# Where ScalarE's and VectorE's share of an activation pair's sums stands in the queue of a fused decoder layer

## The chip, the cores and the metric

The kernel runs on one core of one Trainium2 chip. The metric is the device time of one execution in microseconds (us). A core has five engines with queues of their own, each of which takes its instructions strictly in the order in which the program lists them: TensorE (PE, matrix products), VectorE (DVE), ScalarE (ACT), GpSimd (POOL) and SyncE (SP, which here only issues loads). They wait for each other through semaphores. Transfers between HBM and the on-chip memory run on DMA engines beside them, whoever issues them.

## The reference, cut to what matters

One decoder layer over 272 tokens (16 meta tokens and 256 of the input), model width 2048. The first part projects the input, computes a sparse attention for half of the width and a causal pooling for the other half, mixes both with `w_o` and normalises. The change lies in what follows, a gated feed-forward block (FFN) of width 5632 and a last layer norm:

```python
def conv_gated_ffn(h, w_up, conv_w, conv_b, w_down):
    T = h.shape[1]
    z = h @ w_up
    zp = jnp.pad(z, ((0, 0), (CONV_WIDTH - 1, 0), (0, 0)))
    z = sum(zp[:, j:j + T] * conv_w[j] for j in range(CONV_WIDTH)) + conv_b
    a, g = jnp.split(z, 2, axis=-1)
    return (jax.nn.gelu(a) * g) @ w_down
...
        f = conv_gated_ffn(h, w_up[l], conv_w[l], conv_b[l], w_down[l])
        h = layer_norm(ALPHA * h + f, ln2_g[l], ln2_b[l])
```

Everything is float32.

## The kernel before, in words

**Weights come as blocks.** All weights stream through the kernel as 128 x 2048 blocks of 1 MB, in the order of the list `stream`. `weights()` hands out the block with the index `state["use"]` and first calls `emit` for the blocks up to two ahead of it. `emit` takes a raw buffer (three of them, tag `wraw`) and a split buffer (three, tag `whl`) and calls `fetch` (line 109): SyncE issues the load (L110), and then the block is split into a high and a low half in a shorter float format, in two pieces of 1024 columns. For each piece ACT copies the high half (L123) and DVE subtracts it from the raw block for the low half (L124). A product is then three matmuls for each 128 rows: high x high, high x low and low x high (L187, L188, L189). The load of the block three further on waits until DVE has read the last of the raw buffer; the split of the block three further on waits until PE has done with the split buffer.

**The FFN goes by tiles f = 0 to 43**, each with two halves: half 0 is the value column block `a`, half 1 the gate column block `g`, one weight block each. For f = 0 to 3 (`FOLDED`) the layer norm before the FFN is not yet applied to the activations; it is folded into the product and undone behind it by `unfold` (a DVE copy L707, a DVE product L709, an ACT multiply L711 and a POOL add L712). Then `conv` does the convolution (ACT L699, DVE L700 and L701) and `gate` the activation and the product (ACT L716, DVE L717). From f = 4 on the normalised activations are used.

**The down product** is done with fewer multiplications for parts 0 to 3 and half of part 4: activations and weights are taken in 2 x 2 blocks and seven products of sums replace eight (`seven`). The sums of the weights are made by DVE in `fetch` (L115, L118 to L120). The sums of the activations are made by `forms(r, j, whole)` (from line 729), once for a pair of tiles f: four POOL additions and subtractions into the buffer `forms` (L736 to L739), and then high and low halves of the results by `two_parts`, ACT L722 and DVE L723, four times. A finished pair goes into the list `todo`. At the start of a later tile half, when the block of that half has been handed out, `forms` is called for the first pair in `todo`, if `f > FOLDED - 1 + half_`. So the pairs (0, 1) and (2, 3) are taken at f = 4 half 0 and f = 5 half 0, and each later pair right after its second tile.

**Other work around it.** Behind f = 4 and f = 5, eight DVE transposes each (L861) turn the residual; from f = 6 on, `residual` issues 32 small DMAs from ACT's queue (L693), each of which needs all 16 transposes.

**The end.** The last part (four tiles f) is multiplied plainly, and the row mean of the layer norm comes out of the product itself: each of the last four blocks gets an extra column with the sum of its rows. `row_sums` (line 173) makes it: ACT sums the raw block in place (L176), ACT writes the high half of the sum (L178), DVE the low half (L179). The call for the very last block stands earlier, in the `down` branch. The other three calls stand behind the loop that hands out the last blocks, followed by two ACT sums over `y2`, the running output (L886), one for each half i of the tokens. Then PE makes five pieces for i = 0 and five for i = 1 (L928 to L930); DVE adds each to `y2` (L932); the piece `MEAN` carries the row sums, and L935 makes the negative mean from it. ACT squares follow (L896), DVE subtracts the mean (L902), scales (L917), and the result goes out. The scale and offset rows come as eight loads that POOL issues (L876), each behind a tiny POOL copy (L875) that waits for the last block's load.

**What sets the order.** The program is written in one order, but the framework's scheduler lists the instructions of each engine by priority and readiness as it models them. An instruction that the scheduler thinks ready may therefore be listed ahead of one that the text has before it. Semaphores are added afterwards.

Of the kernel before, what the change touches and what calls it, by code (L numbers as in the profile page):

```python
# [2 lines left out]

# [1 line left out]

# [6 lines left out]
F32 = mybir.dt.float32  # L12
F32R = mybir.dt.float32r
AF = mybir.ActivationFunctionType
ALU = mybir.AluOpType
# [20 lines left out]
FAST = 4  # L36
FOLDED = 4
# [30 lines left out]
def tile_layer(ctx, tc, xt, w_first, w_proj, w_uk, w_uv, w_pool, w_o, w_up, w_down, cols, rows, rel_bias, onehot, out):  # L68
    nc = tc.nc
# [21 lines left out]
    stream = [w_proj[j] for j in range(8)] + [w_uk, w_uv] + [w_proj[j] for j in range(8, 24)]  # L91
    stream += [w_o[j] for j in range(KT)]
    plan = ffn_plan()
    kinds = {}
# [8 lines left out]
            stream.append(w_down[sum(PARTS[:item[1]]) + item[2] * (PARTS[item[1]] // 2) + item[3]])  # L103
    stream += [w_down[d] for d in range(FT - PARTS[-1], FT)]
    spare, last = len(stream) - PARTS[-1], len(stream) - 1
    ready, raws = {}, {}
    state = {"next": 0, "use": 0}

    def fetch(raw, hl, src, kind=None):
        nc.sync.dma_start(raw, src)  # L110
        b11, b12, b21, b22 = (raw[:, c:c + 512] for c in range(0, 2048, 512))
        cuts = (0, 1024, 2048)
        if kind == "A":

            nc.vector.tensor_tensor(b12, b12, b11, op=ALU.subtract)  # L115
        if kind == "B":

            nc.vector.tensor_tensor(b12, b22, b12, op=ALU.subtract)  # L118
            nc.vector.tensor_tensor(b11, b12, b11, op=ALU.add)  # L119
            nc.vector.tensor_tensor(b21, b21, b11, op=ALU.subtract)  # L120
            cuts = (0, 1024, 1536)
        for c in (slice(a, b) for a, b in zip(cuts, cuts[1:])):
            nc.scalar.activation(hl[:, 0, c], raw[:, c], AF.Copy)  # L123
            nc.vector.tensor_tensor(hl[:, 1, c], raw[:, c], hl[:, 0, c].bitcast(F32), op=ALU.subtract)  # L124

    def weight_tiles():
        raw = wp.tile([P, 2048], F32, tag="wraw", name="wraw")
# [2 lines left out]
    def emit(i):  # L130
        if i in ready:
            return
        if i == last:

            raw = wp.tile([P, 2048], F32, tag="wraw", name="wraw")
            nc.sync.dma_start(raw, stream[i])
            raws[i] = raw
            ready[i] = []
            for c in range(0, 2048, 256):
                hl = ring.tile([P, 2, 258], F32R, tag="act", name="whl_r", padded_shape=[P, 2, T])  # L140
                nc.scalar.activation(hl[:, 0, :256], raw[:, c:c + 256], AF.Copy)
                nc.vector.tensor_tensor(hl[:, 1, :256], raw[:, c:c + 256], hl[:, 0, :256].bitcast(F32), op=ALU.subtract)
                ready[i].append(hl)
            return
        if i == spare:
            raw = wp.tile([P, 2048], F32, tag="wraw", name="wraw")
            hl = sb.tile([P, 2, 2048 + 2], F32R, tag="y", name="whl_y")
        else:
            raw, hl = weight_tiles()
        fetch(raw, hl, stream[i], kinds.get(i))  # L150
        ready[i] = hl
        if i >= spare:
            raws[i] = raw
# [6 lines left out]
    def weights(ahead=2):  # L160
        i = state["use"]
        state["use"] += 1
        prefetch(i + 1 + ahead)
        return ready.pop(i)

    def pieces(hl, a, b):

# [5 lines left out]
    def row_sums(i, hl):  # L173

        total = sb.tile([P, 1], F32, name=f"total{i}")
        nc.scalar.activation(raws[i], raws[i], AF.Copy, accum_out=total)  # L176
        hi, lo = (hl[-1][:, p, 256:] if isinstance(hl, list) else hl[:, p, 2048:] for p in range(2))
        nc.scalar.activation(hi, total.to_broadcast([P, 2]), AF.Copy)  # L178
        nc.vector.tensor_tensor(lo, total.to_broadcast([P, 2]), hi.bitcast(F32), op=ALU.subtract)  # L179
# [552 lines left out]
    def forms(r, j, whole):  # L732

        a11, a21, a12, a22 = r[:, 0, :P], r[:, 0, P:], r[:, 1, :P], r[:, 1, P:]
        s = fp.tile([P, 4 * P], F32, name="forms", tag="acc", bufs=1).rearrange("p (a b) -> p a b", b=P)
        nc.gpsimd.tensor_tensor(s[:, 0], a21, a22, op=ALU.add)  # L736
        nc.gpsimd.tensor_tensor(s[:, 2], s[:, 0], a11, op=ALU.subtract)
        nc.gpsimd.tensor_tensor(s[:, 1], a12, s[:, 2], op=ALU.subtract)
        nc.gpsimd.tensor_tensor(s[:, 3], a11, a21, op=ALU.subtract)  # L739
        left = two_parts(slot(), r[:, :, :P])  # L740
        mid = two_parts(slot(), s[:, :2])
        right = ring.tile([P, 2, T], F32R, tag="act", name="right")
        right = two_parts(right[:, :, :2 * P].rearrange("p a (b c) -> p a b c", c=P), s[:, 2:])
        if j % 2 == 0:
            held["lone"], held["other"] = slot(), slot() if whole else None
        two_parts(held["lone"][:, :, j % 2], a22)
        if whole:
            two_parts(held["other"][:, :, j % 2], a21)
        return {"P1": (left, 0), "P2": (left, 1), "P5": (mid, 0), "P3": (mid, 1), "P6": (right, 0),
                "P7": (right, 1), "P4": (held["lone"], j % 2),  # L750
                "a11": (left, 0), "a12": (left, 1), "a21": (held["other"], j % 2), "a22": (held["lone"], j % 2)}
# [44 lines left out]
    for item in plan:  # L796
        if item[0] in "AB":
            seven(*item)
            continue
        if item[0] == "down":  # L800
            _, part, c, g = item
            hl = weights()
            if c == 1:
                emit((last, spare)[g])
                if g == 0:
                    row_sums(last, ready[last])
            if g == 0:
                downs = [big(), big()]
            n = PARTS[part]
            for k in range(4 * g, 4 * g + 4):  # L810
                w = slice(512 * (k - 4 * g), 512 * (k - 4 * g) + 512)
                for i in range(2):
                    a, r = pairs[part][k // 2][f"a{i + 1}{k % 2 + 1}"]
                    nc.tensor.matmul(downs[i], a[:, 0, r], hl[:, 0, w], start=k == 0, stop=False)
                    nc.tensor.matmul(downs[i], a[:, 0, r], hl[:, 1, w], start=False, stop=False)
                    nc.tensor.matmul(downs[i], a[:, 1, r], hl[:, 0, w], start=False, stop=k == n - 1)
            if g == n // 4 - 1:
                for i in range(2):
                    yc = y2[:, i, 512 * c:512 * c + 512]
                    nc.vector.tensor_tensor(yc, yc, downs[i], op=ALU.add)  # L820
            continue
        _, f, half_ = item
        part = next(p for p in range(len(PARTS)) if f < sum(PARTS[:p + 1]))
        if half_ == 0:
            if f % 2 == 0:
                pair = fp.tile([P, 2, S], F32, name="za", tag="z0", bufs=3)
            both = []
        hl = weights()
        ps = big()
        if todo and f > FOLDED - 1 + half_:  # L830
            p, r = todo.pop(0)
            pairs[p].append(forms(r, len(pairs[p]), p == FAST))
        if f < FOLDED:
            k = 0
            if f + half_ == 0:
                product(ps[:, :NE], hl, P, folded, 0, NE, k1=7)
                deviation()
                product(ps[:, :NE], hl, P, folded, 0, NE, k0=7, k1=14)
                deviation_rows()
                k = 14  # L840
            product(ps[:, :NE], hl, P, folded, 0, NE, k0=k)
            while len(h_parts) < min(KT, 3 * (2 * f + half_ + 1)):
                normalise(len(h_parts))
            both.append(ps)
            if half_ == 0:
                continue
            both = [conv(i * FT + f, i, unfold(both[i]), pair[:, f % 2]) for i in range(2)]
        else:
            product(ps[:, :NQ], hl, P, h_parts, 0, NQ)
            both.append(conv(half_ * FT + f, half_, ps, pair[:, f % 2]))  # L850
            if half_ == 0:
                continue
        gate(*both)
        if part > FAST:
            a = fp.tile([P, 2, NE], F32R, name="gp", tag="gp", bufs=16)
            gated.append(two_parts(a[:, :, :S], both[0]))
        elif f % 2:
            todo.append((part, pair))
        if f in (FOLDED, FOLDED + 1):
            for m in range(8 * (f - FOLDED), 8 * (f - FOLDED) + 8):  # L860
                nc.vector.transpose(y[:, m, NM:], y[:, m, NM:])  # L861
        if FOLDED + 2 <= f < FOLDED + 8:
            for _ in range((6, 5, 5)[f % 3]):
                residual(*moves.pop(0))
# [11 lines left out]
            nc.gpsimd.dma_start(t, rows[r:r + 1, 512 * c:512 * c + 512].to_broadcast([P, 512]))  # L876
            gb.append(t)
    order = [0, n - 1] + list(range(1, n - 1))
    for k in range(n - 1):
        row_sums(spare + k, hls[k])  # L880
    MEAN = (1792, 2048 + 2)
    cuts = [[(0, 512), (512, 1024), (1024, 1536), MEAN, (1536, 1792)], [MEAN, (0, 512), (512, 1024), (1024, 1536), (1536, 1792)]]
    mvs = [fp.tile([P, 12], F32, name="mv", tag=f"mv{i}", bufs=1) for i in range(2)]
# [133 lines left out]
```

## Time and profile before

| | us |
|---|---|
| median of 3 runs | 1053.46 |
| lowest and highest run | 1052.87, 1053.99 |
| the profiled execution's own time | 1052.47 |
| its span, first to last instruction | 1050.7 |
| PE busy in the span | 1036.6 (99%) |
| DVE busy | 889.6 (85%) |
| ACT busy | 621.0 (59%) |
| POOL busy | 214.8 (20%) |
| mean granted TensorE clock | 0.997 of full speed |

How to read the rows that follow: a row of the timeline gives the start and the duration in us, the engine, the line of the kernel, the operation, the tile that it writes and those that it reads, shapes where they matter, and in brackets the idle time ahead of it with what ended it. `ACTq` and `SPq` are the queues' own instructions, such as the issue of a DMA. Matmuls overlap, since they are pipelined, so the distance from one start to the next tells more than the duration. A row of the waits gives who waited for whom, the total in us, how often, and the longest.

### The profile page before, as it was taken

Reading aid. Unit: us, or ns where it says so; the run is one execution under the profiler, and the core shown is the slowest. Engines: PE = TensorE matmul, PEld = TensorE weight load, DVE = VectorE, ACT = ScalarE, POOL = GpSimd, SP = SyncE. Lnnn points to the kernel's source line nnn. Section 1 sums busy time; section 2 is a strip of 40 time slices with the busy share of each in tenths; the row PEclk is TensorE's granted clock in tenths of the full one; section 3 lists DMA queues with packets and bytes.
Section 4 is the critical chain, followed back from the end, with each engine's and each line's share of the span. In section 5 each row is a group of like instructions: output and inputs, shape, how many; then the busy total and the mean of one; then the engine's idle time right before and its main releaser. Section 6 shows DMA issues by size and latency. Waiting matters only on the chain. (4 is left out here: it accounts for less than half of the span.)

```text
span 1050.7 us, 19241 instructions
## 1 busy us (share of the span) xinstructions
PE 1036.6 (99%) x7671; PEld 986.5 (94%) x7671; DVE 889.6 (85%) x1381; ACT 621.0 (59%) x998; POOL 214.8 (20%) x264
## 2 busy tenths in 40 slices
PE   9999999999999999999999999999999999999996
PEld 8998999999999999999999999999999999999985
DVE  6879468858779987898989989899898998989876
ACT  7566346745447765565555655556555665556673
POOL 1100014125436231201112011120111221220040
PEclk9999999999999999999999999999999999999998
DMA  8756542454552577998788787887878778787763
GB/s 324 256 170 241 189 152 93 149 188 166 191 199 83 201 221 207 284 311 271 269 288 273 282 276 268 283 278 278 276 268 289 272 279 275 274 284 264 285 218 133
DMA packets 59322, 249.75 MB, mean 238 GB/s; under 512 B 21686, under 2 KB 22112, under 8 KB 32224
## 3 DMA queue, kind: packets, MB, share of 16 engines
q1 hardware_dynamic: 34160, 229.76, 60.3%
q0 software_dynamic: 7600, 15.62, 7.9%
q10 hardware_dynamic: 17472, 3.15, 1.6%
q8 instruction: 60, 0.98, 0.4%
q14 instruction: 30, 0.25, 0.1%
HBM read 232.50 MB, written 2.11 MB: 223 GB/s over the span
## 5 line engine op out<-in xcount | busy, mean ns | idle before, releaser
L124 DVE TENSOR_TENSOR whl<-wraw,whl 128x1024 fp32r<-128x1024 f32 (+1 forms) x416 | 489.6, 1212 | 45.1 <-ACT whl L123 44.5
L123 ACT ACTIVATE whl<-wraw 128x1024 fp32r<-128x1024 f32 (+1 forms) x416 | 402.3, 1015 | 103.5 <-DVE wraw L119 22.5
L188 PE MATMUL mm<-hp,whl 128*128 128x258 f32 x1280 | 362.4, 283 | 0.0
L187 PE MATMUL mm<-hp,whl 128*128 128x258 f32 x1280 | 362.0, 283 | 0.3 <-ACT whl L123 0.3
L189 PE MATMUL mm<-hp,whl 128*128 128x258 f32 x1280 | 361.1, 282 | 0.8 <-DVE whl L124 0.8
L187 PEld LDWEIGHTS mm<-hp,whl 128*128 128x128 f32 x1280 | 242.4, 189 | 3.7 <-ACT whl L123 0.5
L188 PEld LDWEIGHTS mm<-hp,whl 128*128 128x128 f32 x1280 | 242.5, 189 | 3.1
L189 PEld LDWEIGHTS mm<-hp,whl 128*128 128x128 f32 x1280 | 242.9, 190 | 1.0 <-DVE whl L124 1.0
L187 PE MATMUL mm<-xp,whl 128*128 128x256 f32 (+5 forms) x384 | 111.8, 291 | 0.0
L188 PE MATMUL mm<-xp,whl 128*128 128x256 f32 (+5 forms) x384 | 108.9, 284 | 0.0
L189 PE MATMUL mm<-xp,whl 128*128 128x256 f32 (+5 forms) x384 | 108.7, 283 | 0.0
L699 ACT ACTIVATE z<-mm,cv 128x256 f32<-128x256 f32 x40 | 22.6, 565 | 97.3 <-PE mm L189 96.4
L188 PEld LDWEIGHTS mm<-xp,whl 128*128 128x128 f32 x384 | 72.3, 188 | 0.8 <-issue 0.5
L187 PEld LDWEIGHTS mm<-xp,whl 128*128 128x128 f32 x384 | 72.4, 189 | 0.6
L189 PEld LDWEIGHTS mm<-xp,whl 128*128 128x128 f32 x384 | 72.4, 189 | 0.3 <-DVE whl L124 0.2
L739 POOL TENSOR_TENSOR forms<-za 128x128 f32<-128x128 f32 x20 | 26.4, 1321 | 219.4 <-DVE za L717 211.9
L765 PE MATMUL at<-whl,gp 128*128 128x512 f32 x180 | 71.2, 395 | 0.0
L766 PE MATMUL at<-whl,gp 128*128 128x512 f32 x180 | 71.1, 395 | 0.0
L764 PE MATMUL at<-whl,gp 128*128 128x512 f32 x180 | 71.1, 395 | 0.0
L699 ACT ACTIVATE za<-mm,cv 128x256 f32<-128x256 f32 x40 | 22.5, 564 | 67.4 <-PE mm L189 67.4
L736 POOL TENSOR_TENSOR forms<-za 128x128 f32<-128x128 f32 x20 | 21.8, 1088 | 106.4 <-DVE za L717 106.3
L766 PEld LDWEIGHTS at<-whl,gp 128*128 128x128 f32 x180 | 33.8, 188 | 8.0
(327 smaller groups left out, 1942.2 us busy)
## 6 DMA issues: line engine op xcount, KB each, us to landing
wraw<-in_w_up SPq DMA_DIRECT2D x88, 1024.0 KB, 5.1
wraw<-in_w_down SPq DMA_DIRECT2D x80, 1024.0 KB, 6.3
wraw<-in_w_proj SPq DMA_DIRECT2D x24, 1024.0 KB, 5.0
wraw<-in_w_o SPq DMA_DIRECT2D x16, 1024.0 KB, 4.9
y<-v POOLq DMA_DIRECT2D x27, 256.0 KB, 8.3
y<-u POOLq DMA_DIRECT2D x18, 256.0 KB, 4.7
wraw<-in_w_first SPq DMA_DIRECT2D x8, 304.0 KB, 5.5
x<-in_xt SPq DMA_DIRECT2D x1, 2176.0 KB, 8.6
```

What stands on the lines that cost most here:

```text
L123: nc.scalar.activation(hl[:, 0, c], raw[:, c], AF.Copy)
L124: nc.vector.tensor_tensor(hl[:, 1, c], raw[:, c], hl[:, 0, c].bitcast(F32), op=ALU.subtract)
L187: nc.tensor.matmul(ps, wh, ah, start=n == 0, stop=False)
L188: nc.tensor.matmul(ps, wh, al, start=False, stop=False)
L189: nc.tensor.matmul(ps, wl, ah, start=False, stop=n == KT - 1)
L699: nc.scalar.activation(z, src[:, 2:NQ], AF.Identity, bias=col(C_B, j), scale=col(C_W, 3 * j + 2))
L736: nc.gpsimd.tensor_tensor(s[:, 0], a21, a22, op=ALU.add)
L739: nc.gpsimd.tensor_tensor(s[:, 3], a11, a21, op=ALU.subtract)
L764: nc.tensor.matmul(ps, a[:, 0, i], hl[:, 0, w], start=j == 0, stop=False)
L765: nc.tensor.matmul(ps, a[:, 0, i], hl[:, 1, w], start=False, stop=False)
L766: nc.tensor.matmul(ps, a[:, 1, i], hl[:, 0, w], start=False, stop=j == n - 1)
```

## The change

`fetch` returns the last ACT and the last DVE instruction of a split, and `emit` keeps them for each block in `split`. A new context `behind(i)` makes every ACT instruction traced in it be listed after that ACT instruction of block i, and every DVE instruction after that DVE instruction; this is an order in the queues alone and adds no semaphore. `forms` is called within `behind(state["use"])`, so behind the split of the block that the next tile half will use, and the condition for it becomes `f > FOLDED + half_`. The three calls of `row_sums` at the end stand within `behind(spare + n - 2)`, the last block that is split in whole pieces.

```diff
             nc.vector.tensor_tensor(b21, b21, b11, op=ALU.subtract)
             cuts = (0, 1024, 1536)
         for c in (slice(a, b) for a, b in zip(cuts, cuts[1:])):
-            nc.scalar.activation(hl[:, 0, c], raw[:, c], AF.Copy)
-            nc.vector.tensor_tensor(hl[:, 1, c], raw[:, c], hl[:, 0, c].bitcast(F32), op=ALU.subtract)
+            upper = nc.scalar.activation(hl[:, 0, c], raw[:, c], AF.Copy)
+            lower = nc.vector.tensor_tensor(hl[:, 1, c], raw[:, c], hl[:, 0, c].bitcast(F32), op=ALU.subtract)
+        return upper, lower
...
-        fetch(raw, hl, stream[i], kinds.get(i))
+        split[i] = fetch(raw, hl, stream[i], kinds.get(i))
...
+    @contextmanager
+    def behind(i):
+
+        upper, lower = (getattr(ins, "ins", ins) for ins in split[i])
+        with tc.issue_after(upper), tc.issue_after(lower):
+            yield
...
-        if todo and f > FOLDED - 1 + half_:
+        if todo and f > FOLDED + half_:
             p, r = todo.pop(0)
-            pairs[p].append(forms(r, len(pairs[p]), p == FAST))
+            with behind(state["use"]):
+                pairs[p].append(forms(r, len(pairs[p]), p == FAST))
...
-    for k in range(n - 1):
-        row_sums(spare + k, hls[k])
+    with behind(spare + n - 2):
+        for k in range(n - 1):
+            row_sums(spare + k, hls[k])
```

The lists of PE and of SyncE stay as they are, instruction for instruction. ACT's and DVE's lists hold the same work in another order, in these places:

- Pair (0, 1): its four ACT and four DVE instructions stood around the split of the block for f = 5 half 0; they now stand behind the split of the block for f = 5 half 1. Pair (2, 3): it stood on both sides of the split for f = 5 half 1; it now stands behind the split for f = 6 half 1.
- The last DVE transpose (L861) moves ahead, to the place that the first low half (L723) had ahead of the split for f = 5 half 0. The first two residual DMAs (L693) move ahead of the ACT split for f = 5 half 1, and the last of the 32 moves ahead by one tile half.
- In POOL's list two additions of pair (2, 3) change places, and one output accumulation (L789) of part 0 moves behind three POOL additions. On DVE, in part 0, L786 (which frees a PSUM bank of `seven`) moves behind a split and an L772, and three splits change places with a neighbour.
- Two 128 x 128 high and low halves of part 4's pairs move behind the next split.
- At the end ACT's list was: split of block 1 of the last four, L176 of it, split of block 2, L178, split of block 3, L176, L886, L178, L176, L886, L178. It becomes: split 1, split 2, split 3, then L176, L176, L178, L176, L178, L886, L178, L886. On DVE the low halves of the sums (L179) change places with the first additions L932 accordingly.

More of the change, by code (lines that the diff above doesn't have):

```diff
@@ L1 @@
 import math
[L2 removed]
+from contextlib import ExitStack, contextmanager
 import numpy as np
```

3 lines of the change are left out of this document (1 added, 2 removed).

## The prediction

> **What bounds the kernel now.** I read the page first, then the windows, PE's waits, and the timeline around each wait.
>
> ```profile
> span 1050.7 us, 19241 instructions
> ```
> ```profile
> 500.00:600.00 100.00, 100.00 (x719) 94.55 (x718) 92.52 (x129) 58.69 (x83) 16.17 (x19) 1.00 0.81 278
> ```
> ```profile
> PE mm L189 <- DVE whl L124: 1.2, 2, 0.8
> ```
>
> PE bounds everything up to the last 30 us, in this stretch without a gap and at full granted clock (1.00). PE's list doesn't change, so a change of ACT's and DVE's order is worth only what PE waits for, or what it makes PE wait for. PE's waits on low halves come to 1.2 us in this view, which is short, because a pipelined matmul counts as busy until its modelled end. The distance between starts shows the loss. Only two places hold such a loss near the instructions that move: the block for f = 5 half 1, and the last four blocks.
>
> ```profile
> 374.06 0.29 PE L188 MATMUL mm<-hp,whl 128*128 128x258 f32 x1
> 374.19 0.28 PE L189 MATMUL mm<-hp,whl 128*128 128x258 f32 x1
> 374.74 0.39 PE L187 MATMUL mm<-hp,whl 128*128 128x258 f32 x1 [0.27 <-ACT whl L123]
> 374.97 0.28 PE L188 MATMUL mm<-hp,whl 128*128 128x258 f32 x1
> 376.06 0.39 PE L189 MATMUL mm<-hp,whl 128*128 128x258 f32 x1 [0.82 <-DVE whl L124]
> 376.29 0.28 PE L187 MATMUL mm<-hp,whl 128*128 128x258 f32 x1
> ```
>
> Undisturbed starts are 0.12 us apart. From 374.19 to 376.29 four steps took 2.10 us instead of 0.48: 1.62 us are lost. First the high half is late, then the low half.
>
> **Part 1: the pairs (0, 1) and (2, 3).** Why was that split late? Here are ACT's, DVE's and POOL's timelines.
>
> ```profile
> 367.93 0.60 ACT L699 ACTIVATE z<-u,cv 128x256 f32<-128x256 f32 x1 [0.78 <-POOL u L712]
> 370.88 0.42 ACT L722 ACTIVATE gp<-forms 128x256 fp32r<-128x256 f32 x1 [2.35 <-POOL forms L738]
> ...
> 372.86 0.42 ACT L722 ACTIVATE gp<-za 128x256 fp32r<-128x256 f32 x1 [1.05 <-DVE za L717]
> 373.19 0.55 ACT L699 ACTIVATE za<-mm,cv 128x256 f32<-128x256 f32 x1
> 373.64 2.00 ACT L123 ACTIVATE whl<-wraw 128x1024 fp32r<-128x1024 f32 x2
> 374.92 0.73 ACTq L693 DMA_DIRECT2D y<-x  x1
> ```
> ```profile
> 368.90 0.68 DVE L700 SCALAR_TENSOR_TENSOR z<-u,cv,z 128x256 f32<-128x256 f32 x1
> 371.34 0.42 DVE L723 TENSOR_TENSOR gp<-forms,gp 128x256 fp32r<-128x256 f32 x1 [1.75 <-ACT gp L722]
> 371.68 0.48 DVE L701 SCALAR_TENSOR_TENSOR z<-u,cv,z 128x256 f32<-128x256 f32 x1
> ...
> 372.41 0.42 DVE L717 TENSOR_TENSOR za<-za,z 128x256 f32<-128x256 f32 x1
> ...
> 374.79 2.35 DVE L124 TENSOR_TENSOR whl<-wraw,whl 128x1024 fp32r<-128x1024 f32 x2
> ```
> ```profile
> 367.97 1.32 POOL L736 TENSOR_TENSOR forms<-za 128x128 f32<-128x128 f32 x1
> 370.39 0.46 POOL L738 TENSOR_TENSOR forms<-za,forms 128x128 f32<-128x128 f32 x1
> ```
>
> ACT stood 2.35 us behind POOL's four sums, with the split queued behind; DVE stood 1.75 us for the same cause, and ACT another 1.05 us behind DVE. The block itself was in long before: its load was issued at 357.68 and took 4.9 us.
>
> ```profile
> 357.68 11.65 SPq L110 DMA_DIRECT2D wraw<-in_w_up  x3
> ```
> ```profile
> DMA to landing us min/median/max: 4.9/4.9/4.9
> ```
>
> In the changed list, what follows z's L699 on ACT (done at 368.53) is two residual issues, L699 for the next tile, then the split. Two issues are 2 x 0.73 from 367.95 on, until 369.4. The L699 takes 0.55, so the high half starts at about 369.9 instead of 373.64 and is done by 371.9. DVE goes on from L700 at 368.90: L700 0.68, L701 about 0.5, L717 0.4, L700 and L701 for the next tile 1.0, so the low half starts at about 371.5, takes 2.35 and ends at 373.9; its first half is ready at 372.7. PE wants the high half at 374.31, the first low half at 374.55, the second low half 2.9 us later. Margin 1.9 us or more on each: the 1.62 us go.
>
> POOL's sums of this pair now run beside that DVE chain. The L700 beside L736 took 0.68, the L701 beside no POOL work 0.48. The Trainium skill, GPSIMD Engine Reference, Specifications, says that GpSimd shares its SBUF interfaces with VectorE and collides with instructions of two SBUF inputs, and the 0.68 agrees. By that rule the four DVE steps beside POOL get 0.2 us each longer, 0.8 in all; by the undisturbed row nothing. Either way the margin holds, and the gain is 1.62.
>
> What is queued behind the moved work? The eight instructions of pair (0, 1) now follow this split and precede z's L699 for f = 4 half 1 and the split for f = 6 half 0. Four ACT steps of 0.3 to 0.4 us delay that ACT split to about 374.0, four DVE steps delay its low half to about 375.8 to 378.6; PE wants it at 374.31 + 5.76 = 380.1 (48 steps of 0.12). Pair (2, 3) follows the split for f = 6 half 1, with one block more of margin. Its consumers, `seven` of part 0, start 30 us later. I cost all this at nothing: the cover is the block that PE still has to work through, and without it the price would be DVE's 4 x 0.34 = 1.4 us once per pair. The other swaps in part 0 and part 4 exchange neighbours of 0.3 to 1.2 us in a stretch where PE lost nothing; also nothing.
>
> **Part 2: the end.**
>
> ```profile
> 1015.83 2.00 ACT L123 ACTIVATE whl<-wraw 128x1024 fp32r<-128x1024 f32 x2
> 1017.72 0.20 ACT L178 ACTIVATE whl_y<-total 128x2 fp32r<-128x2 f32 x1
> 1017.82 2.00 ACT L123 ACTIVATE whl<-wraw 128x1024 fp32r<-128x1024 f32 x2
> 1019.71 1.91 ACT L176 ACTIVATE wraw<-wraw 128x2048 f32<-128x2048 f32 x1
> ...
> 1021.61 1.91 ACT L886 ACTIVATE y<-y 128x2048 f32<-128x2048 f32 x1
> ```
> ```profile
> 1023.64 0.69 DVE L932 TENSOR_TENSOR y<-y,mm 128x512 f32<-128x512 f32 x1 [0.80 <-ACT y L886]
> ...
> 1027.62 0.16 DVE L179 TENSOR_TENSOR whl<-total,whl 128x2 fp32r<-128x2 f32 x1 [2.62 <-ACT whl L178]
> ...
> 1028.72 0.21 DVE L935 TENSOR_SCALAR mv<-mm,mv 128x1 f32<-128x1 f32 x1
> ...
> 1037.54 1.27 DVE L932 TENSOR_TENSOR y<-y,at 128x512 f32<-128x512 f32 x2
> ```
> ```profile
> 1019.95 0.40 PE L928 MATMUL mm<-whl,gp 128*128 128x512 f32 x1
> ...
> 1020.82 0.39 PE L930 MATMUL mm<-whl,gp 128*128 128x512 f32 x1
> 1021.05 0.39 PE L928 MATMUL mm<-whl_y,gp 128*128 128x512 f32 x1
> ...
> 1028.06 0.29 PE L930 MATMUL mm<-whl,gp 128*128 128x258 f32 x1
> ```
> ```profile
> 1016.42 4.05 POOL L875 COPY gb<-wraw 128x1 f32<-128x1 f32 x8 [14.40 <-DMA wraw<-in_w_down]
> ```
> ```profile
> DMA to landing us min/median/max: 8.9/8.9/8.9
> ```
>
> Here PE no longer decides. From L935 at 1028.72 on, ACT's squares and DVE's additions run one behind the other to the end, so only an earlier L935 helps. L935 had two bounds, nearly level: the last MEAN matmul ends at 1028.06 + 0.29 = 1028.35, and DVE came through L179 at 1027.62, behind ACT's last sum.
>
> In the old frame of time the new ACT list gives this. The last split waits for its load, which took 8.9 us and landed at 1016.3, just ahead of the POOL copy that waits for it. High half 1016.35 to 1018.25, then three L176 at the 1.90 between 1019.71 and 1021.61 and two L178 at the 0.10 between 1017.72 and 1017.82: L886 starts at 1018.25 + 5.7 + 0.2 = 1024.15. It lets go of `y2` 2.0 later, as it did between 1021.61 and 1023.64: 1026.15. The first L932 must wait for it. Then three L932 of 512 columns at 0.64 (two took 1.27) and one of 256 at half of that: 2.24, L935 at about 1028.4. That is 0.32 us earlier than 1028.72. PE gains more there: from 1019.95 to 1020.82 two steps took 0.87 where an undisturbed one takes 0.23 (1020.82 to 1021.05), so 0.41 go, and some 0.1 on row sums that came late, an estimate from L179 at 1027.62 beside the last MEAN matmul at 1028.06. PE would let L935 come 0.5 earlier, but ACT's list holds it. I take 0.32, because ACT's steps are all rows of this trace. Ends of the range: 0.5 gained, or a loss if the load lands later, since the reserve of 1.5 us that the old order had (1017.82 against 1016.3) is gone.
>
> **Sum.** 1.62 + 0.32 = 1.94 us. Everything between the two places is paced by PE and moves along with it. The profiled execution took 1052.47 (1050.7 of span and 1.77 around it); it was 0.99 quicker than the median, 1053.46. PE's work is the same in every execution, so the slower ones wait more, and some of that falls on the removed waits: I add 0.1 of it and take 2.06 against the median, 1051.4 us. That lies 0.04 us inside 0.2%, 2.1 us, which is about what a measurement of this kernel can tell from no change.
>
> **The rivals.**
> - *More than the sum.* L935 comes at PE's bound, 1.62 + 0.5 = 2.12, and a typical execution carries up to all of the 0.99 us in the places that go: 3.11 us, 1050.3. For it: DVE and ACT stood behind POOL, whose spans vary (L736 took 1.32, L738 0.46). Against it: nothing shows where the 0.99 us lie.
> - *The wait comes back.* The change doesn't do what it says: another wait takes the place at f = 5 or the end eats it. The longest landing of a weight load is the measure.
>
> ```profile
> DMA to landing us min/median/max: 4.6/5.4/10.6
> ```
>
> With 10.6 instead of 8.9 us for the last block L935 is 1.7 later: 1.62 + 0.32 - 1.7 = 0.24, 1053.2. The Trainium skill, DMA: Bandwidth & Descriptors, Issuing engines are not separate DMA queues, says that loads of all issuing engines run on the same 16 DMA engines and interleave. By that rule POOL's output accumulations lengthen this load, the 8.9 against a median of 5.4 agrees, and the time would be the 1053.2 just given.
> - *Slower.* The same place, further: each us that the last block lands later costs one, since three sums and L886 (7.9 us of ACT) stand behind its split ahead of the first L932. From 1.94 us late the kernel is no faster, from 4.0 us late it is slower by 0.2% (2.1 us); at 5 us late 1053.46 + 3.1 = 1056.5. Against it: the longest landing is 1.7 above this one.
>
> **How the numbers follow.** The sum as worked, 1.3 to 2.7 us: 0.72, of which 0.42 beyond the 2.1 and 0.30 within, since the median execution waits more than the profiled one. More than the sum: 0.13. The wait comes back: 0.07. Slower: 0.08. So faster 0.55, the same 0.37, slower 0.08. The range goes from the first rival's 1050.3 to 1053.1, just short of the second's.
>
> **What would show it.** Right: PE's starts around the block for f = 5 half 1 0.12 apart; ACT's split there about 3.7 us earlier, ahead of L722; no gap at L929 in the last blocks; L886 behind three L176, and the first L932 waiting for it longer than 0.80. Wrong: a new PE wait on L123 or L124 between f = 6 and the end, L935 not earlier relative to PE, or a landing of the last block that holds up ACT's split.

## The result and the profile after

The changed kernel took 1050.91 us in the median of 10 runs (1050.0 to 1052.27), the kernel before 1053.26 beside it (1052.34 to 1054.86, 10 runs). The ratio is 0.9976, with a 95% interval from 0.9969 to 0.9984: 2.35 us less, or 0.22%, so faster, by about the 0.2% that can be told from no change (the interval goes from 0.16% to 0.31%). A second comparison of the same two kernels (e5 below) gave 0.9972 (0.9962 to 0.9982), 3.08 us less. The forecast was 1051.4.

The profiled execution of the changed kernel took 1050.0 us, 2.47 less than that of the kernel before. The span on its page:

```profile
span 1048.2 us, 19242 instructions
```

In the changed kernel the added lines shift the numbers: L123, L124 and L110 are as before, L187 to L189 became L195 to L197, L176, L178 and L179 became L184, L186 and L187, L722 and L723 became L730 and L731, L886 became L896, L896 became L906, L902 became L912, L928 to L930 became L938 to L940, L932 became L942, and L935 became L945. The kernels of the experiments have some of these lines up to three further up or down.

**The block for f = 5 half 1.** PE's timeline where four steps took 2.10 us before:

```profile
374.06 0.29 PE L196 MATMUL mm<-hp,whl 128*128 128x258 f32 x1
374.18 0.28 PE L197 MATMUL mm<-hp,whl 128*128 128x258 f32 x1
374.30 0.28 PE L195 MATMUL mm<-hp,whl 128*128 128x258 f32 x1
374.42 0.28 PE L196 MATMUL mm<-hp,whl 128*128 128x258 f32 x1
374.54 0.28 PE L197 MATMUL mm<-hp,whl 128*128 128x258 f32 x1
```

The starts are 0.12 us apart: the stall has gone. ACT's and DVE's timelines show why:

```profile
367.92 1.40 ACTq L701 DMA_DIRECT2D y<-x  x2
369.37 0.57 ACT L707 ACTIVATE za<-mm,cv 128x256 f32<-128x256 f32 x1 [0.85 <-DVE whl L124]
369.84 2.01 ACT L123 ACTIVATE whl<-wraw 128x1024 fp32r<-128x1024 f32 x2
...
372.04 0.41 ACT L730 ACTIVATE gp<-za 128x256 fp32r<-128x256 f32 x1
...
373.62 1.06 ACT L123 ACTIVATE whl<-wraw 128x1024 fp32r<-128x1024 f32 x1
```
```profile
368.88 0.68 DVE L708 SCALAR_TENSOR_TENSOR z<-u,cv,z 128x256 f32<-128x256 f32 x1
369.60 0.56 DVE L709 SCALAR_TENSOR_TENSOR z<-u,cv,z 128x256 f32<-128x256 f32 x1
370.20 0.57 DVE L725 TENSOR_TENSOR za<-za,z 128x256 f32<-128x256 f32 x1
...
371.60 2.35 DVE L124 TENSOR_TENSOR whl<-wraw,whl 128x1024 fp32r<-128x1024 f32 x2
373.87 0.42 DVE L731 TENSOR_TENSOR gp<-za,gp 128x256 fp32r<-128x256 f32 x1
...
375.99 1.50 DVE L124 TENSOR_TENSOR whl<-wraw,whl 128x1024 fp32r<-128x1024 f32 x1
```

The split now starts at 369.84 on ACT (373.64 before) and at 371.60 on DVE (374.79 before). The pair's sums (L730, L731), which wait for POOL, come behind it. (The bracket at L707 names DVE; it is the two DMA issues on ACT's queue that run to 369.32 just ahead of it, as the prediction had it.)

**The end.** ACT's and DVE's timelines from the last split on:

```profile
1014.40 2.01 ACT L123 ACTIVATE whl<-wraw 128x1024 fp32r<-128x1024 f32 x2 [0.50 <-DMA wraw<-in_w_down]
1016.32 1.90 ACT L184 ACTIVATE wraw<-wraw 128x2048 f32<-128x2048 f32 x1
...
1022.19 1.90 ACT L896 ACTIVATE y<-y 128x2048 f32<-128x2048 f32 x1
...
1026.89 0.72 ACT L906 ACTIVATE sq<-y,mv 128x512 f32<-128x512 f32 x1 [0.72 <-DVE mv L945]
1027.51 0.19 ACT L906 ACTIVATION_READ_ACCUMULATOR sq<-y,mv 128x1 f32 x1
```
```profile
1024.21 0.69 DVE L942 TENSOR_TENSOR y<-y,mm 128x512 f32<-128x512 f32 x1 [1.74 <-ACT y L896]
...
1024.88 1.78 DVE L942 TENSOR_TENSOR y<-y,mm 128x512 f32<-128x512 f32 x3
1026.58 0.21 DVE L945 TENSOR_SCALAR mv<-mm,mv 128x1 f32<-128x1 f32 x1
1027.79 0.75 DVE L912 SCALAR_TENSOR_TENSOR y<-y,mv,gb 128x512 f32<-128x512 f32 x1 [1.00 <-issue]
```

The last split waits 0.50 us for its load, the first addition 1.74 for ACT's sum over `y2` (0.80 before), and L945 starts at 1026.58 (1028.72 before): 2.14 us earlier, of which 1.61 came along with PE. From L945 to the end of the span the changed kernel took 21.63 us, the kernel before 21.97. So three terms make the 2.48 us between the two traces: 1.61 at f = 5 half 1, 0.53 up to L945, 0.34 behind it. The prediction had the first two, as 1.62 and 0.32, and not the third.

### The profile page after: what moved, and what is told of

It reads as the page before. It is cut to its first block, busy times and chain, and to the rows that moved or that the text cites. A ratio compares the mean times of both kernels' runs of the same rounds, so it can differ in the third digit from the quotient of the medians.

```text
span 1048.2 us, 19242 instructions
## 1 busy us (share of the span) xinstructions
PE 1035.8 (99%) x7671; PEld 986.4 (94%) x7671; DVE 890.0 (85%) x1381; ACT 621.3 (59%) x998; POOL 212.4 (20%) x264
## 5 line engine op out<-in xcount | busy, mean ns | idle before, releaser
L124 DVE TENSOR_TENSOR whl<-wraw,whl 128x1024 fp32r<-128x1024 f32 (+1 forms) x416 | 489.5, 1212 | 43.3 <-ACT whl L123 42.6
L123 ACT ACTIVATE whl<-wraw 128x1024 fp32r<-128x1024 f32 (+1 forms) x416 | 402.5, 1015 | 114.8 <-DVE wraw L119 28.5
L195 PE MATMUL mm<-hp,whl 128*128 128x258 f32 x1280 | 361.9, 283 | 0.0
L197 PE MATMUL mm<-hp,whl 128*128 128x258 f32 x1280 | 361.0, 282 | 0.0
L195 PEld LDWEIGHTS mm<-hp,whl 128*128 128x128 f32 x1280 | 242.4, 189 | 3.2
L197 PEld LDWEIGHTS mm<-hp,whl 128*128 128x128 f32 x1280 | 242.9, 190 | 0.0
L195 PE MATMUL mm<-xp,whl 128*128 128x256 f32 (+5 forms) x384 | 111.8, 291 | 0.0
L197 PE MATMUL mm<-xp,whl 128*128 128x256 f32 (+5 forms) x384 | 108.7, 283 | 0.0
L707 ACT ACTIVATE z<-mm,cv 128x256 f32<-128x256 f32 x40 | 22.6, 565 | 93.9 <-PE mm L197 93.5
L195 PEld LDWEIGHTS mm<-xp,whl 128*128 128x128 f32 x384 | 72.4, 189 | 0.6
L197 PEld LDWEIGHTS mm<-xp,whl 128*128 128x128 f32 x384 | 72.4, 189 | 0.3 <-DVE whl L124 0.2
L772 PE MATMUL at<-whl,gp 128*128 128x512 f32 x180 | 71.1, 395 | 0.0
L707 ACT ACTIVATE za<-mm,cv 128x256 f32<-128x256 f32 x40 | 22.6, 565 | 62.5 <-PE mm L197 61.7
L115 DVE TENSOR_TENSOR wraw<-wraw 128x512 f32<-128x512 f32 x36 | 24.7, 685 | 19.8 <-DMA wraw<-in_w_down 19.8
```

The costliest lines, as they stand in the source:

```text
L123: upper = nc.scalar.activation(hl[:, 0, c], raw[:, c], AF.Copy)
L124: lower = nc.vector.tensor_tensor(hl[:, 1, c], raw[:, c], hl[:, 0, c].bitcast(F32), op=ALU.subtract)
L195: nc.tensor.matmul(ps, wh, ah, start=n == 0, stop=False)
L197: nc.tensor.matmul(ps, wl, ah, start=False, stop=n == KT - 1)
L707: nc.scalar.activation(z, src[:, 2:NQ], AF.Identity, bias=col(C_B, j), scale=col(C_W, 3 * j + 2))
L772: nc.tensor.matmul(ps, a[:, 0, i], hl[:, 0, w], start=j == 0, stop=False)
```

## One table for all runs

The spans of single executions can't be compared as they are, since they differ before anything that the change touches. The profile has one fixed place for each kernel, PE's column sums ahead of the FFN; here in the kernel before and in e8 below:

```profile
308.71 0.55 PE L234 MATMUL at<-ones,sums 128*128 128x64 f32 x4
```
```profile
310.55 0.33 PE L242 MATMUL at<-ones,sums 128*128 128x64 f32 x2
```

I take this start as zero in each trace. All columns are in us; e1 to e10 are told below. "PE at the end" is PE's first matmul of the last four blocks; "load took" and "landed" are those of the last block's load, the second against PE's first matmul of the end, as are L945 (by the numbering of the changed kernel) and "first split", where ACT begins to split the first of the last four blocks (tile `whl_y`). By "the last block" I mean the one whose load is issued last.

| | zero | PE at the end, from zero | first split | load took | landed | L945 | L945 to the end | zero to the end |
|---|---|---|---|---|---|---|---|---|
| before | 308.71 | 709.13 | -7.42 | 8.89 | -1.56 | 10.88 | 21.97 | 741.98 |
| changed | 308.71 | 707.52 | -6.86 | 8.22 | -1.91 | 10.35 | 21.63 | 739.50 |
| e1 part 1 alone | 309.00 | 707.53 | -7.21 | 9.03 | -1.32 | 11.08 | 21.55 | 740.16 |
| e2 part 2 alone | 310.06 | 709.15 | -7.45 | 8.92 | -1.52 | 10.57 | 21.95 | 741.68 |
| e3 tie alone | 308.81 | 708.91 | -7.41 | 8.90 | -1.53 | 10.87 | 21.90 | 741.69 |
| e4 first sum over y2 ahead | 309.42 | 707.53 | -5.86 | 9.48 | -0.95 | 12.06 | 21.75 | 741.34 |
| e5 changed again | 308.90 | 707.51 | -6.30 | 9.32 | -1.13 | 10.96 | 21.57 | 740.03 |
| e6 normalise later | 308.89 | 707.13 | -7.50 | 8.14 | -1.56 | 10.53 | 21.62 | 739.27 |
| e7 one more on DVE | 308.57 | 707.52 | -6.70 | 8.11 | -1.80 | 10.35 | 21.94 | 739.81 |
| e8 two more on DVE | 310.55 | 707.53 | -7.39 | 8.53 | -1.83 | 10.35 | 21.66 | 739.53 |
| e9 before, one more | 309.03 | 709.13 | -7.57 | 8.48 | -1.95 | 10.72 | 21.51 | 741.37 |
| e10 transposes later | 309.21 | 706.99 | -7.15 | 8.18 | -2.19 | 10.35 | 21.62 | 738.96 |

PE's place at the end repeats to 0.02 us among kernels that have the same lists up to there. So the spread between executions sits at the start, up to 2 us by the zeros, and at the end, in the landings.

## The experiments

**e1 and e2: each part alone.** e1 leaves out the second edit of this pair, e2 the first:

```diff
-        if todo and f > FOLDED - 1 + half_:
+        if todo and f > FOLDED + half_:
             p, r = todo.pop(0)
-            pairs[p].append(forms(r, len(pairs[p]), p == FAST))
+            with behind(state["use"]):
+                pairs[p].append(forms(r, len(pairs[p]), p == FAST))
...
-    for k in range(n - 1):
-        row_sums(spare + k, hls[k])
+    with behind(spare + n - 2):
+        for k in range(n - 1):
+            row_sums(spare + k, hls[k])
```

> Part 1 alone; the three row sums stand where they stood before. Theory (the gain of part 1 is PE's stall at f = 5 half 1 and nothing else): PE starts 0.12 us apart there, and everything behind comes 1.62 us earlier, the end included: minus 1.6 us against the kernel before, between 1.2 and 2.0; ACT still sums y2 behind two row sums, and the first addition of the end waits about 0.8 us as before. Rival (all of the gain comes from the end): the same time as before, within 0.4 us. Rival (the load of the last block comes 0.3 earlier by part 1): minus 1.9.

> Part 2 alone; the pairs stand where they stood before. Theory by the prediction's steps: the stall of 1.6 us at f = 5 half 1 stays, L945 comes 0.3 us earlier against PE's matmuls before it: minus 0.3 us. If all that the changed kernel gained beyond 1.62 belongs to this part (0.2 more up to L945 and 0.3 behind it): minus 0.8 to 0.9. Rival (the row sums hold up the end, three sums ahead of the first sum over y2): plus 0.2 to plus 1.7.

e1 took 1051.71 against 1053.09 (ratio 0.9984, 0.9975 to 0.9993), e2 1052.88 against the same (0.9998, 0.9989 to 1.0007). In the table e1 has the whole 1.60 us of PE's stall and e2 none of it; e2 has L945 0.31 nearer to PE's first matmul at the end than the kernel before, with a landing that differs by 0.04. These are the two terms of the prediction, each by itself. In times part 1 is shown and part 2, at 0.3 us, lies within its interval.

e1's end came 0.20 later against PE than that of the kernel before. Both have the old order at the end. ACT's timeline at the first of the last four blocks, in the kernel before, then in e1:

```profile
1010.43 2.01 ACT L123 ACTIVATE whl_y<-wraw 128x1024 fp32r<-128x1024 f32 x2 [3.24 <-DMA wraw<-in_w_down]
1013.91 1.92 ACT L176 ACTIVATE wraw<-wraw 128x2048 f32<-128x2048 f32 x1 [1.48 <-DVE whl_y L124]
```
```profile
1009.33 2.01 ACT L123 ACTIVATE whl_y<-wraw 128x1024 fp32r<-128x1024 f32 x2 [3.35 <-DMA wraw<-in_w_down]
1012.82 1.92 ACT L184 ACTIVATE wraw<-wraw 128x2048 f32<-128x2048 f32 x1 [1.48 <-DVE whl_y L124]
```

This split waits for its load, its row sum waits for the split's low half, and from there ACT has no gap up to the last row sum. L945 follows the start of this split by 18.27 to 18.29 us in all four traces with the old order (before, e1, e3, e9). In e1 it began 0.21 later against PE, and L945 came 0.20 later. The last block's landing decides nothing in this order: its split began 1.51 to 1.78 us after it in the same four traces. PE stood longer for the low half of that split as well:

```profile
1018.64 0.40 PE L937 MATMUL mm<-whl,gp 128*128 128x512 f32 x1
1019.42 0.50 PE L938 MATMUL mm<-whl,gp 128*128 128x512 f32 x1 [0.38 <-DVE whl L124]
```

So the old order did have the reserve of 1.5 us against a late last landing that the prediction read into ACT's list. It had none against a late landing of the first of the four blocks.

**e3: only the tie.** The condition `f > FOLDED - 1 + half_` stays, `with behind(state["use"])` is added, and the row sums stand as before.

> Only the tie: each pair's sums behind the split of the next block, but with the old condition, so POOL's sums and their tile are those of before; row sums as before. Theory (what counts is that the split for f = 5 half 1 no longer stands behind work that waits for POOL): PE's stall there goes, minus 1.6 us, between 1.2 and 2.0, as with the whole of part 1. Rival (the pair has to be taken a tile later, since POOL's sums beside the split hold up DVE): at least half of the stall stays, 0 to minus 0.8 us.

It took 1053.35 against 1053.09 (1.0002, 0.9993 to 1.0011): no gain. The rival's outcome came true, but not for its reason. ACT's, DVE's and PE's timelines:

```profile
371.00 0.42 ACT L730 ACTIVATE gp<-forms 128x256 fp32r<-128x256 f32 x1 [2.36 <-POOL forms L746]
...
372.28 2.00 ACT L123 ACTIVATE whl<-wraw 128x1024 fp32r<-128x1024 f32 x2
```
```profile
371.45 0.43 DVE L731 TENSOR_TENSOR gp<-forms,gp 128x256 fp32r<-128x256 f32 x1 [1.77 <-ACT gp L730]
...
374.57 2.46 DVE L124 TENSOR_TENSOR whl<-wraw,whl 128x1024 fp32r<-128x1024 f32 x2
```
```profile
374.52 0.28 PE L196 MATMUL mm<-hp,whl 128*128 128x258 f32 x1
375.96 0.39 PE L197 MATMUL mm<-hp,whl 128*128 128x258 f32 x1 [1.15 <-DVE whl L124]
```

With the tie alone pair (2, 3) goes behind the split, and ACT's high half comes at 372.28, in time. But pair (0, 1) is tied to an earlier split and still stands ahead of this one. ACT waits 2.36 us for POOL's sums of that pair, DVE 1.77 for ACT, and the low half starts at 374.57 instead of 374.79: PE loses 1.42 of the 1.62 us as before. It isn't POOL's sums running beside the split, as the rival had it, but work ahead of the split that waits for them. The other half of the edit does nothing by itself either: with the new condition and no tie the lists of all five engines are those of the kernel before, instruction for instruction. The two lines of part 1 work only together: the tie makes the pair follow a split, and the condition picks the split that stood behind POOL's sums.

**e4: the first sum over `y2` ahead of two row sums.**

```diff
+    mvs = [fp.tile([P, 12], F32, name="mv", tag=f"mv{i}", bufs=1) for i in range(2)]
     with behind(spare + n - 2):
+        nc.scalar.activation(y2[:, 0], y2[:, 0], AF.Copy, accum_out=mvs[0][:, 0:1])
         for k in range(n - 1):
             row_sums(spare + k, hls[k])
+        nc.scalar.activation(y2[:, 1], y2[:, 1], AF.Copy, accum_out=mvs[1][:, 0:1])
...
-    mvs = [fp.tile([P, 12], F32, name="mv", tag=f"mv{i}", bufs=1) for i in range(2)]
-
-    for i in range(2):
-        nc.scalar.activation(y2[:, i], y2[:, i], AF.Copy, accum_out=mvs[i][:, 0:1])
```

In ACT's list the first sum over `y2` came behind one row sum (L184) and ahead of the other two.

> The changed kernel, with ACT's sum over the first half of y2 ahead of the second and third row sum. Theory (ACT's list, three row sums ahead of the first sum over y2, holds L945): the first sum over y2 ends near 1020.2 instead of 1026.2, the first addition of the end no longer waits 1.7 us for it, and L945 comes at PE's bound, 0.3 us earlier (1026.2 instead of 1026.6): minus 2.65 against the kernel before, and 0.3 less than the changed kernel. Rival (PE then waits for the row sums, whose last one comes 2 us later): a wait of PE on a row sum ahead of the MEAN piece, L945 no earlier or up to 1.5 us later, minus 2.35 to minus 0.9.

It took 1051.88 against 1053.09 (0.9987, 0.9978 to 0.9995), a smaller gain than that of the changed kernel. PE's timeline in the MEAN piece (L937 and L939 are L938 and L940 of the changed kernel):

```profile
1026.69 0.28 PE L939 MATMUL mm<-whl_y,gp 128*128 128x256 f32 x1
1027.89 0.38 PE L937 MATMUL mm<-whl,gp 128*128 128x258 f32 x1 [0.93 <-ACT whl L186]
```

PE stood 1.08 us longer than a step of 0.12 for a row sum; the rival was right. The load was late in this execution too (9.48 us). By the rule that e5 gives below, a landing at -0.95 puts L945 at 11.14 in the order of the changed kernel; it came at 12.06, so this order costs 0.9 us: PE needs the row sums sooner than DVE needs the sum over `y2`.

**e5: the changed kernel once more.**

> The changed kernel a second time, unchanged. Its first profile had the last block's load in 8.2 us; the same loads took 8.9 to 9.5 in the other kernels. Theory (behind the last split ACT has no reserve left, so L945 follows this landing one for one): L945 comes 12.3 us after the landing again, whatever the load takes, so with 8.9 us it comes 0.7 later against PE's matmuls than in the first profile. Rival (the end keeps a reserve, as in the kernel before): L945 at the same distance from PE's first matmul of the last four blocks, 10.35 us, with another landing. Time: minus 2.3 against the kernel before, between 1.6 and 2.9, by both.

1050.71 against 1053.79 (0.9972, 0.9962 to 0.9982). This profile has the load that the first one hadn't, 9.32 us. ACT's and DVE's timelines at the end:

```profile
1015.36 2.01 ACT L123 ACTIVATE whl<-wraw 128x1024 fp32r<-128x1024 f32 x2 [0.42 <-DMA wraw<-in_w_down]
...
1023.14 1.90 ACT L896 ACTIVATE y<-y 128x2048 f32<-128x2048 f32 x1
```
```profile
1025.17 0.69 DVE L942 TENSOR_TENSOR y<-y,mm 128x512 f32<-128x512 f32 x1 [1.73 <-ACT y L896]
...
1027.37 0.21 DVE L945 TENSOR_SCALAR mv<-mm,mv 128x1 f32<-128x1 f32 x1
```

L945 came at 10.96 instead of 10.35. Read over the table, the order of the changed kernel puts L945 12.09 us behind the last landing (e2 -1.52 and 10.57, e6 -1.56 and 10.53, e5 -1.13 and 10.96), and never before 10.35, where PE's matmuls hold it (changed, e7, e8, e10, landings from -1.80 to -2.19). So the theory holds for late landings, with a floor at PE's pace for early ones. Its rival, that a reserve is left, is wrong.

The old order goes by another landing, that of the first of the four blocks, as told at e1. In the kernel before, e1 and e3 the two landings lie nearly as far apart, so that L945 also seems to follow the last one by 12.40 to 12.44 us; e9, with 12.67 to the last landing and 18.29 to the first split, tells the two apart.

What part 2 is worth therefore depends on both landings. With those of the kernel before it is 0.31 us (e2). With 18.28 us behind the first split, the old order would have put L945 at 11.42 in the first profile of the changed kernel, at 11.98 in e5, and at 10.78 to 11.58 in e6, e7, e8 and e10. Against the L945 of the table that makes part 2 worth 0.25 to 1.23 us in these executions. This is an estimate from the traces; no run shows it directly. The 0.53 of the first profile are therefore no measure of the order alone: the last block landed 0.35 earlier there than in the kernel before, and the first split began 0.56 later.

**e7, e8 and e9: the third of a microsecond behind L945.** Between ACT's first sum of squares and the first L912 the kernel before left a gap that the changed one doesn't have. e7 adds one VectorE instruction to the changed kernel, e8 two, e9 one to the kernel before; nothing else in any list changes.

```diff
     nc.vector.memset(st, 1.0)
+    extra = fp.tile([P, 4], F32, name="extra", bufs=1)
+    nc.vector.memset(extra[:, 0:1], 0.0)
```

The places named in these expectations count VectorE's list with runs of equal instructions as one.

> The changed kernel, with one tiny VectorE memset more, 700 us ahead of the end. In the profiles so far the first subtraction of the mean (L912) started 0.09 us after ACT's sum of squares ended in two kernels, and 0.45 after it in three others. Theory (its place in VectorE's list decides: 1272 in the two, 1271 or 1273 in the three): 0.45, and the end 0.35 us later against L945. Rival (something else decides, such as what the engine waits for): 0.09 as in the changed kernel.

> The same with two memsets. Theory (the place in the list decides, in turns of two): 0.09 again. Theory (the place decides, a longer turn): 0.45. Rival (something else decides): 0.09 here and with one memset.

> The kernel before, with one tiny VectorE memset more, 700 us ahead of the end; no other list changes. Theory (the first subtraction of the mean starts 0.36 us earlier or later by its place in VectorE's list alone, and the kernel before had the bad place): 0.09 us after ACT's sum of squares instead of 0.45, the end 0.35 us nearer to L935, about minus 0.35 us. Rival (the 0.36 us belong to the moved pairs): 0.45 as before, the same time.

ACT's sum of squares and DVE's first subtraction of the mean in the kernel before:

```profile
1029.59 0.19 ACT L896 ACTIVATION_READ_ACCUMULATOR sq<-y,mv 128x1 f32 x1
```
```profile
1030.24 0.75 DVE L902 SCALAR_TENSOR_TENSOR y<-y,mv,gb 128x512 f32<-128x512 f32 x1 [1.31 <-issue]
```

The same in e7 (where L906, L912 and L945 have become L908, L914 and L947), then in e9 (L896 and L902 have become L898 and L904):

```profile
1026.74 0.72 ACT L908 ACTIVATE sq<-y,mv 128x512 f32<-128x512 f32 x1 [0.61 <-DVE mv L947]
1027.37 0.19 ACT L908 ACTIVATION_READ_ACCUMULATOR sq<-y,mv 128x1 f32 x1
```
```profile
1028.02 0.75 DVE L914 SCALAR_TENSOR_TENSOR y<-y,mv,gb 128x512 f32<-128x512 f32 x1 [1.37 <-issue]
```
```profile
1029.76 0.19 ACT L898 ACTIVATION_READ_ACCUMULATOR sq<-y,mv 128x1 f32 x1
```
```profile
1030.04 0.75 DVE L904 SCALAR_TENSOR_TENSOR y<-y,mv,gb 128x512 f32<-128x512 f32 x1 [0.94 <-issue]
```

In the kernel before DVE starts 0.46 us after ACT's row sum of squares ends (1029.78 to 1030.24), in e7 too (1027.56 to 1028.02); in e9 0.09 (1029.95 to 1030.04), as in e8. The column from L945 to the end says the same: 21.94 in e7, 21.66 in e8, 21.51 in e9, against 21.97 before and 21.63 changed. So the third term of the gain, 0.34 us, is no effect of the order itself. It goes by the place of that instruction in VectorE's list. Counted in the traces together with the semaphore instructions, it is the 1600th in all five with 0.44 to 0.46 us (before, e2, e3, e4, e7), and the 1599th, 1601st or 1602nd in the seven with 0.09. So it is one single place, and not a turn of two, by which e10 (1602nd) would be late. The changed kernel and e1 have the instruction one place earlier because they have one semaphore instruction less ahead of it, which came along with part 1. A memset does as much for the kernel before. The tile `extra` isn't the cause, since e7 and e8 both have it. In times it doesn't show: e9 took 1053.28 against 1053.32 (1.0002, 0.9993 to 1.0011), and 0.36 us is less than that interval resolves; e7 and e8 have one time each, 1050.15 and 1051.86, and their difference is that of their zeros, 1.98, less the 0.28 that e8 gains.

**e6 and e10: the same remedy at the next two stalls.** In both kernels PE still stalls at f = 2 half 1 and f = 3 half 1. e6 ties `normalise` at f = 2, and e10 also the transposes that then moved ahead of the split:

```diff
-            while len(h_parts) < min(KT, 3 * (2 * f + half_ + 1)):
-                normalise(len(h_parts))
+            with behind(state["use"] + 1) if f > 1 else ExitStack():
+                while len(h_parts) < min(KT, 3 * (2 * f + half_ + 1)):
+                    normalise(len(h_parts))
...
-            for m in range(8 * (f - FOLDED), 8 * (f - FOLDED) + 8):
-                nc.vector.transpose(y[:, m, NM:], y[:, m, NM:])
+            with behind(state["use"] - 5):
+                for m in range(8 * (f - FOLDED), 8 * (f - FOLDED) + 8):
+                    nc.vector.transpose(y[:, m, NM:], y[:, m, NM:])
```

> The changed kernel, with the same tie once more: ACT's and DVE's share of normalise at f = 2 stands behind the split of two blocks on. Theory (what a split waits for in the queue decides, as at f = 5 half 1): PE's two stalls at f = 2 half 1 and f = 3 half 1, 0.56 + 0.11 and 0.23 + 0.11 us, go: minus 1.0 against the changed kernel, minus 3.3 against the kernel before. Rival (the work that was ahead now holds up a later split, of f = 3 half 0 or f = 4 half 0): a new stall of PE between 344 and 365 us, and less than 0.4 us gained against the changed kernel.

> The kernel of e6, with the DVE transposes of the residual tied behind the split for f = 2 half 1 (they had been pulled ahead of it when normalise was tied). Theory (DVE's low half for f = 2 half 1 stood behind four transposes): that low half starts when ACT's first high half is done, 338.2 instead of 338.45, and PE's remaining stall there, 0.51 + 0.10, falls by 0.2 to 0.3 us: minus 0.25 against e6. ACT's high half, which starts at 337.2, holds the rest. Rival (the transposes now stand ahead of a later split): a new stall, no gain.

PE's and DVE's timelines in e6 (L871 are the transposes):

```profile
339.05 0.28 PE L196 MATMUL mm<-fold,whl 128*128 128x260 f32 x1
339.68 0.39 PE L197 MATMUL mm<-fold,whl 128*128 128x260 f32 x1 [0.35 <-DVE whl L124]
```
```profile
337.76 0.76 DVE L871 STREAM_TRANSPOSE x<-x 128x256 f32<-128x256 f32 x2
338.45 2.31 DVE L124 TENSOR_TENSOR whl<-wraw,whl 128x1024 fp32r<-128x1024 f32 x2
```

e6 removed the second stall (PE at the end 0.39 us earlier than in the changed kernel) and kept the first, 0.51 of 0.56 us: what stood ahead of that split came from earlier calls of `normalise`, which the edit doesn't move, and the scheduler put four transposes into the place on DVE. With the transposes tied too (e10), that stall falls to 0.37 and PE comes 0.53 earlier than in the changed kernel. Expected were 1.0 and 1.25 us in all, so the direction was right and the size less than half; no new stall came up, so the rivals' reason was wrong as well. In times e6 took 1050.34 against 1053.79 (0.9971, 0.9960 to 0.9981) and e10 1050.23 against 1053.32 (0.9975, 0.9966 to 0.9985). Both medians are lower than the changed kernel's, but the 0.4 and 0.5 us to it are shown by the traces alone.

## Why the prediction was right, point by point

- *The stall at f = 5 half 1, 1.62 us.* Right to 0.02: the loss is 1.62 or 1.63 us in the three traces that have it whole (before, e2, e9), and gone in every kernel with part 1. ACT's split started at 369.84 (369.9 foreseen), DVE's low half at 371.60 (371.5), the next splits at 373.62 and 375.99 (374.0 and 375.8). The cause that it named, ACT and DVE standing behind POOL's sums, is shown by e3, where the wait stayed and with it 1.42 us of the stall.
- *DVE beside POOL.* The extra time was 0.08 us for L709 (0.56, undisturbed 0.48) and 0.15 for L725 (0.57, undisturbed 0.42), beside the 0.68 of L708 that was there before. The rule that the prediction quoted from the Trainium skill (GPSIMD Engine Reference, Specifications) is borne out in kind; the 0.2 that the prediction put on each of four steps was too much, and the margin covered it.
- *Part 2, 0.32 us.* Right for landings like those of the trace that it was worked out from: 0.31 (e2). The first L942 waited longer, as foreseen. That PE would allow 0.5 was right as well: with an early last landing L945 came 0.53 earlier, at PE's pace.
- *"The reserve ... is gone".* Right. The old order began the last split 1.51 to 1.78 us after its landing; in the new one L945 follows that landing one for one (e5), which is the mechanism of the second and third rivals. A landing late enough for their prices was not seen. What the prediction overlooked is that the old order followed the first of the four landings as strictly (e1), which the new one does not.
- *A sign of being wrong that came true.* "A landing of the last block that holds up ACT's split" did occur: the split waits 0.50 us for its load in the first profile. It says nothing against the sum, which itself had the split begin at the landing.
- *Why the last load took 8.9 us.* The prediction put this down to POOL's output accumulations. The last of them was indeed in flight, issued at 1000.8 and 10.6 us long, but the load also ran beside that of the block before, issued 0.42 us earlier (1006.98 and 1007.40). No run separates the two.
- *The 0.1 us for slower executions, and the first rival's 0.99.* No run shows either at f = 5 half 1, where the stall is the same in the three traces that have it whole. At the end there may be something of the kind, since part 2 is worth more where the first of the four blocks lands late; the size is only estimated (e5).
- *What was missed.* 0.34 us behind L945, by the place of an instruction in VectorE's list. It isn't in the sum of 1.94; with it and the early last landing the profiled difference is 2.48. That it fell on the side of the gain is luck.
- *The forecast.* 1.94 by traces, 2.06 against the median (1.94 and 0.1 are 2.04; the rest is the rounding to 1051.4); measured were 2.35 in the first comparison, 0.25 beyond the 2.1 that the forecast had taken as the bound of what can be told, and 3.08 in the second. The intervals go from 1.7 to 3.3 and from 1.9 to 4.0 us, so the times alone don't tell the sum from the rival *More than the sum*. The traces bear out the sum's two terms, but not that they are all: the parts alone gained 1.38 and 0.21 in times, less together than the whole change, which fits a part 2 worth more in some executions without proving it.

## What to carry to other kernels

Where one engine is busy 99% of the span, look at the distance between its starts, and at each long one ask what stands ahead of the late producer in its own queue: here a split stood behind small work that waited for a third engine. Moving such work behind the next thing that the bounding engine needs pays exactly the stall, but check in the list that it has really passed the producer, since the tie and the later tile each did next to nothing alone. And before a gain of a few tenths is put down to an edit, take out of the comparison what differs between executions anyway, here the start and the landings at the end.

## What the runs showed of the hardware that was not expected

- The first L912 starts 0.09 us or some 0.45 us after the ACT instruction that it waits for, by its place in VectorE's list: late as the 1600th instruction, five traces of five, and not as the 1599th, 1601st or 1602nd, seven of seven. One instruction more turned 0.09 into 0.46 (e7) and 0.46 into 0.09 (e9). The profile puts the wait down to "issue". Why is open. The Trainium skill (Runtime: NRT & Kernel Launch, Instruction fetch mechanics) says that instructions are fetched ahead in blocks of 256 and that this is mostly hidden. Whether the end of such a block lies at this place no run here shows.
- The load of the last block, 1 MB, took from 8.11 to 9.48 us in five executions whose lists up to it are the same but for a memset or two (changed, e4, e5, e7, e8). With the changed order, where it lands later than some 1.74 us ahead of PE's first matmul of the end, L945 and with it the end come later one for one (12.09 less 10.35).
- The load of the first of the last four blocks took 8.06 to 9.70 us in the eight kernels with part 1, and 7.99 to 8.15 in the four without it or with its tie alone. Whether part 1 is the cause no run shows.
